# One level of Strassen's scheme in the down projection of a decoder layer, with the sums of operands made by accumulating DMAs

## The chip, the core and the metric

The kernel runs on one core of one Trainium2 chip. TensorE (PE in the rows, PEld for its weight loads) multiplies, VectorE (DVE), ScalarE (ACT) and GpSimd (POOL) do elementwise work, and 16 DMA engines move data for the queues of SyncE (SP), ACT and POOL. The metric is the device time of one execution in microseconds; lower is better. A measurement of this kernel tells two versions apart from about 0.5% on.

## The reference, cut to what matters

One layer: a mixer with three head groups, then a SwiGLU feed-forward network, then a final norm (its gain `norm_final`, one row per token). The change touches the feed-forward network's second product, with 512 tokens, width 1024 and `FFN_HIDDEN` 2816:

```
x = x + mix @ w_out
h = rmsnorm(x, norm_ffn)
gate, up = jnp.split(h @ w_gate_up, 2, axis=-1)
return x + (jax.nn.silu(gate) * up) @ w_down
```

Everything is float32.

## The kernel before

**Precision by splitting.** Each float32 operand of a large product is split into a high part `hi` (cast by ACT) and a rest `lo` (subtracted by DVE or POOL), and each product is three matmuls: hi·hi, hi·lo, lo·hi. Weights arrive as chunks of 256 rows by up to 512 columns (512 KB); `split` makes `hi` and `lo` of a chunk, from a ring of four buffers each, and `chunk()` keeps `LOOK` = 3 chunks split ahead of the one that TensorE uses.

**Stages.** The input projection and the mixer come first (to about 440 us), then the output projection (to about 480 us), then the gate and up projection (to 707.7 us), then the down projection with the final norm. The gate and up projection already runs as seven products of halves for each of six column blocks (five of 512 columns, one of 256). Its sums of weights are made partly by DVE, partly by DMAs that add what they bring to what stands in the destination (`add_chunk`, `accum_op=ALU.add`, issued on POOL's queue). When a buffer of the last block's weights comes free, `follow` brings a chunk of the down projection into it (`bring`, SP's queue): twelve buffers, `down_units`.

**Down projection before.** The activations, transposed by `turn` into 22 tiles `aT` of 128 rows by 512 tokens, are split by ACT and POOL (`split_t`). The loop runs over 11 chunk pairs in `DOWN_ORDER` and, inside, over four groups of 128 tokens; each step does twelve matmuls into two of eight PSUM banks (two column halves, two row tiles, three matmuls). The banks are first seeded with the residual `x2` by transposes. At the last chunk pair each token group is finished: square and sum on ACT, reciprocal root on POOL (`rsq`), scaling, and store. Four activation tiles are kept in DRAM (`ad`) for lack of room, and `x2` is brought back from DRAM (`x2d`) during the last gate and up block.

The order of instructions on each engine is settled by a scheduler at build time, not by the order of the code alone. Each engine, and each DMA queue's issuing engine, runs its own list in order: an instruction that waits holds up all that stand behind it on that engine.

Of the kernel before, what the change touches and what calls it, by code (L numbers as in the profile page):

```python
# [8 lines left out]
F32 = mybir.dt.float32  # L9
F32R = mybir.dt.float32r  # L10
# [6 lines left out]
P = 128  # L17
# [72 lines left out]
DOWN_ORDER = [2, 3, 4, 5, 6, 7, 8, 9, 10, 0, 1]  # L90
SPILL = 4
for _kc in DOWN_ORDER:
    for _g in range(2):
        CHUNKS.append(("down", 256 * _kc, np.arange(512 * _g, 512 * _g + 512)))
# [25 lines left out]
def trunk(tc, x, xt, wcat, vecs, rows, consts, posn, gfin, out):  # L120
# [6 lines left out]
    with contextlib.ExitStack() as es:  # L127
# [41 lines left out]
        for _, _, c in CHUNKS:  # L169
            offsets.append(o)  # L170
            o += P * 2 * len(c)
# [8 lines left out]

        def bring(i, t):

            w = len(CHUNKS[i][2])
            raw = t[:, 0:2 * w]
            sp.dma_start(
                out=raw,
                in_=wcat[offsets[i]:offsets[i] + P * 2 * w].rearrange("(p f) -> p f", p=P),
            )
            raws[i] = raw

        def add_chunk(i, t):

            w = len(CHUNKS[i][2])
            pool.dma_start(  # L194
                out=t[:, 0:2 * w],
                in_=wcat[offsets[i]:offsets[i] + P * 2 * w].rearrange("(p f) -> p f", p=P),
                accum_op=ALU.add,
            )
# [8 lines left out]
        def split(raw, eng, first=False):  # L207
# [5 lines left out]
            return v3(hi, 2), v3(lo, 2)  # L213
# [716 lines left out]

        def begin_ffn():
# [11 lines left out]
            def pair_jobs(p, U):  # L943
# [19 lines left out]
                def follow(unit, quarter=None):  # L963

                    if p + 1 < len(GU_W):
                        if quarter is not None:
                            gload(p + 1, quarter, unit)
                    else:
                        for t in unit:
                            down_units.append(t)  # L970
                            bring(DN0 + len(down_units) - 1, t)
# [40 lines left out]
            def down_job(j):  # L1012
                def run():
                    r_ = split(raws[DN0 + j], dve)
                    if DN0 + j + 12 < len(CHUNKS):
                        bring(DN0 + j + 12, down_units[j % 12])
                    return r_

                return run
# [5 lines left out]
            jobs.extend(down_job(j) for j in range(len(CHUNKS) - DN0))  # L1025
# [180 lines left out]
        aT = [None] * (2 * len(DOWN_ORDER))  # L1206
# [15 lines left out]
        def turn(p, f, a):  # L1222


            def go():
# [3 lines left out]
                kt = 4 * p + f  # L1229
                t = slot()  # L1230
                act.copy(out=t, in_=ps)
                if kt < SPILL:
                    sp.dma_start(out=ad[kt], in_=t)
                else:
                    aT[kt] = t
# [8 lines left out]
        for p, w in enumerate(GU_W):  # L1244
# [15 lines left out]
            if last:  # L1260
                for k in range(KD):
                    x2[k] = slot()
                    sp.dma_start(out=x2[k], in_=x2d[k])
# [12 lines left out]
            if last:  # L1276
                for hf in range(2):
                    gf[hf] = slot()
                    sp.dma_start(out=gf[hf], in_=gfin[512 * hf:512 * hf + 512].partition_broadcast(P))
# [19 lines left out]
        for k in range(SPILL):  # L1299
            aT[k] = slot()  # L1300
            sp.dma_start(out=aT[k], in_=ad[k])
        banks = [bank() for _ in range(4)]
        NK2 = len(DOWN_ORDER)
        asp = {}

        def split_t(n):
            if n < NK2:
                for kk in (2 * DOWN_ORDER[n], 2 * DOWN_ORDER[n] + 1):
                    hi, lo = slot(F32R), slot(F32R)
                    act.copy(out=hi, in_=aT[kk])  # L1310
                    pool.tensor_tensor(out=lo, in0=aT[kk], in1=hi.bitcast(F32), op=ALU.subtract)
                    asp[kk] = hi, lo

        split_t(0)
        split_t(1)


        order = [(n, c) for n in range(NK2) for c in range(NC)]
        order[3:5] = [(1, 0), (0, 3)]
        w2s = {}  # L1320
        for n, c in order:
            kc = DOWN_ORDER[n]
            if n not in w2s:
                w2s[n] = [chunk(), chunk()]
                split_t(n + 2)
            w2 = w2s[n]
            if n == 0 and c >= 2:
                banks += [mbank() for _ in range(2)]
            for hf in range(2):
                whi, wlo = w2[hf]  # L1330
                o_ = banks[2 * c + hf]
                if n == 0:
                    for k in range(4):
                        mm(o_[:, k * P:(k + 1) * P], lhsT=x2[4 * hf + k][:, c * P:(c + 1) * P], rhs=ident, start=k == 0, stop=False, is_transpose=True)
                for k in range(2):
                    ah, al = (t[:, c * P:(c + 1) * P] for t in asp[2 * kc + k])
                    mm(o_, lhsT=ah, rhs=whi[:, k, :], start=False, stop=False)  # L1337
                    mm(o_, lhsT=ah, rhs=wlo[:, k, :], start=False, stop=False)  # L1338
                    mm(o_, lhsT=al, rhs=whi[:, k, :], start=False, stop=n == NK2 - 1 and k == 1)  # L1339
            while (n, c) == (0, 2) and tail:  # L1340
                turn_one()
            if n == NK2 - 1:
                ss, rf = small(2, "ssf", bufs=4), small(1, "rf", bufs=4)
                t = [slot() for _ in range(2)]
                for hf in range(2):
                    o_ = banks[2 * c + hf]
                    act.activation(out=t[hf], in_=o_, func=AF.Square, accum_out=ss[:, hf:hf + 1])
                pool.tensor_scalar(out=ss[:, 0:1], in0=ss[:, 0:1], scalar1=1.0 / D, scalar2=EPS, op0=ALU.mult, op1=ALU.add)
                dve.scalar_tensor_tensor(out=rf, in0=ss[:, 1:2], scalar=1.0 / D, in1=ss[:, 0:1], op0=ALU.mult, op1=ALU.add)
                rsq(rf)  # L1350
                for hf in range(2):
                    y = slot()
                    dve.tensor_tensor(out=y, in0=banks[2 * c + hf], in1=gf[hf], op=ALU.mult)
                    if hf == 0:
                        act.activation(out=y, in_=y, func=AF.Copy, scale=rf)
                    else:
                        dve.tensor_scalar(out=y, in0=y, scalar1=rf, scalar2=None, op0=ALU.mult)
                    (act if hf else sp).dma_start(out=out[c, :, 512 * hf:512 * hf + 512], in_=y)
# [70 lines left out]
```

## Time and profile before

| | us |
|---|---|
| median of three runs (lowest to highest) | 840.64 (839.98 to 843.13) |
| the profiled execution | 839.7 |
| its span in the trace | 837.9 |
| TensorE busy | 825.2 |
| VectorE busy | 531.6 |
| ScalarE busy | 384.3 |
| GpSimd busy | 235.1 |

The span is the time from the first to the last instruction in the trace; the profiled execution's own time is 1.8 us longer than it. Matmuls overlap in their pipeline, so what one costs is the distance between the starts of two, not its recorded duration.

### The profile page before, as it was taken

Reading aid. Unit: us, or ns where it says so; the run is one execution under the profiler, and the core shown is the slowest. Engines: PE = TensorE matmul, PEld = TensorE weight load, DVE = VectorE, ACT = ScalarE, POOL = GpSimd, SP = SyncE. Lnnn points to the kernel's source line nnn. Section 1 sums busy time; section 2 is a strip of 40 time slices with the busy share of each in tenths; the row PEclk is TensorE's granted clock in tenths of the full one; section 3 lists DMA queues with packets and bytes.
Section 4 is the critical chain, followed back from the end, with each engine's and each line's share of the span. In section 5 each row is a group of like instructions: output and inputs, shape, how many; then the busy total and the mean of one; then the engine's idle time right before and its main releaser. Section 6 shows DMA issues by size and latency. Waiting matters only on the chain.

```text
span 837.9 us, 11283 instructions
## 1 busy us (share of the span) xinstructions
PE 825.2 (98%) x4238; PEld 711.0 (85%) x4238; DVE 531.6 (63%) x767; ACT 384.3 (46%) x659; POOL 235.1 (28%) x250
## 2 busy tenths in 40 slices
PE   9999999999999999999999999999999999999997
PEld 9989889898978788888888878888888889888885
DVE  6648757594839878556732797887878777422223
ACT  6344536463445454244422584646455557612223
POOL 3234524242012966531700221000010103850001
PEclk9999999999999999999999999999999999999999
DMA  7423242232313423213923579496665459330002
GB/s 256 158 60 125 83 141 87 95 113 65 125 63 91 147 77 126 76 59 116 328 76 106 158 228 262 132 270 176 185 188 143 99 151 388 114 118 0 1 1 100
DMA packets 38262, 110.72 MB, mean 132 GB/s; under 512 B 4392, under 2 KB 4776, under 8 KB 38208
## 3 DMA queue, kind: packets, MB, share of 16 engines
q1 hardware_dynamic: 33744, 96.93, 34.0%
q0 software_dynamic: 3456, 11.54, 7.7%
q10 hardware_dynamic: 1008, 1.54, 0.5%
q8 instruction: 33, 0.54, 0.3%
q14 instruction: 21, 0.17, 0.1%
HBM read 104.70 MB, written 5.29 MB: 131 GB/s over the span
## 4 chain that ended last, share of the span: by engine, by line
PE 62%; DVE 6%; POOL 1%; issue 1%; ACT 1%; DMA 0%; POOLq 0%; SPq 0%
PE b L1218 6%; PE b L1219 6%; PE b L1217 6%; PE b L428 4%; PE b L427 4%; PE b L429 4%; PE b L409 3%; PE b L411 3%; PE b L410 3%; PE b L1337 2%; PE b L1338 2%; PE b L1339 2%; PE m L1337 2%; PE m L1338 2%; PE m L1339 2%; PE m L1217 2%
## 5 line engine op out<-in xcount | busy, mean ns | idle before, releaser
L212 DVE TENSOR_TENSOR lo<-raw,hi 128x1024 fp32r<-128x1024 f32 (+3 forms) x97 | 117.2, 1212 | 116.5 <-ACT hi L211 116.0
L211 ACT CAST hi<-raw 128x1024 fp32r<-128x1024 f32 (+3 forms) x106 | 103.3, 977 | 155.1 <-PE b L428 75.8
L212 DVE TENSOR_TENSOR lo<-big,hi 128x1024 fp32r<-128x1024 f32 (+1 forms) x79 | 96.9, 1230 | 87.7 <-ACT hi L211 86.3
L211 ACT CAST hi<-big 128x1024 fp32r<-128x1024 f32 (+1 forms) x79 | 78.1, 991 | 112.8 <-PE m L1339 54.5
L427 PE MATMUL b<-s,hi 128*128 128x512 f32 x304 | 120.1, 396 | 0.8 <-ACT s L677 0.8
L428 PE MATMUL b<-s,hi 128*128 128x512 f32 x304 | 119.0, 392 | 0.0
L429 PE MATMUL b<-s,lo 128*128 128x512 f32 x304 | 118.5, 392 | 0.0
L410 PE MATMUL b<-lo,s 128*128 128x384 f32 (+2 forms) x320 | 115.3, 360 | 0.2 <-DVE lo L212 0.2
L409 PE MATMUL b<-hi,s 128*128 128x384 f32 (+2 forms) x320 | 114.1, 365 | 0.0
L411 PE MATMUL b<-hi,s 128*128 128x384 f32 (+2 forms) x320 | 113.6, 361 | 0.0
L1218 PE MATMUL b<-lo,s 128*128 128x512 f32 (+1 forms) x240 | 89.7, 374 | 1.2 <-DVE lo L212 1.2
L1219 PE MATMUL b<-hi,s 128*128 128x512 f32 (+1 forms) x240 | 89.3, 372 | 0.0
L1217 PE MATMUL b<-hi,s 128*128 128x512 f32 (+1 forms) x240 | 88.4, 378 | 0.0
L427 PEld LDWEIGHTS b<-s,hi 128*128 128x128 f32 x304 | 57.1, 188 | 12.1 <-ACT s L677 1.1
L429 PEld LDWEIGHTS b<-s,lo 128*128 128x128 f32 x304 | 57.1, 188 | 11.6
L428 PEld LDWEIGHTS b<-s,hi 128*128 128x128 f32 x304 | 57.2, 188 | 11.0
L410 PEld LDWEIGHTS b<-lo,s 128*128 128x128 f32 x320 | 60.2, 188 | 5.4 <-DVE lo L212 0.6
L409 PEld LDWEIGHTS b<-hi,s 128*128 128x128 f32 x320 | 60.1, 188 | 4.7 <-issue 0.2
L411 PEld LDWEIGHTS b<-hi,s 128*128 128x128 f32 x320 | 60.0, 188 | 4.9
L658 DVE SCALAR_TENSOR_TENSOR s<-s,vec,s 128x511 f32<-128x511 f32 (+2 forms) x66 | 58.5, 929 | 0.2 <-ACT s L655 0.2
L194 POOL DMA_DIRECT2D big<-in_wcat x19 | 16.8, 882 | 145.1 <-DMA big<-in_wcat 116.9
L1218 PEld LDWEIGHTS b<-lo,s 128*128 128x128 f32 x240 | 45.2, 189 | 9.4 <-DVE lo L212 1.6
(293 smaller groups left out, 1536.2 us busy)
## 6 DMA issues: line engine op xcount, KB each, us to landing
raw<-in_wcat SPq DMA_DIRECT2D x70, 512.0 KB, 3.4
big<-in_wcat SPq DMA_DIRECT2D x54, 512.0 KB, 4.4
big<-in_wcat POOLq DMA_DIRECT2D x17, 512.0 KB, 7.6
raw<-in_wcat SPq DMA_DIRECT2D x20, 384.0 KB, 3.1
s<-in_xt SPq DMA_DIRECT2D x16, 256.0 KB, 6.7
s<-mdr SPq DMA_DIRECT2D x12, 256.0 KB, 4.2
s<-adr SPq DMA_DIRECT2D x12, 256.0 KB, 5.0
x2d<-s SPq DMA_DIRECT2D x8, 256.0 KB, 3.2
```

The source lines that it names most:

```text
L211: pin(act.copy(out=hi, in_=raw), first)
L212: pin(eng.tensor_tensor(out=lo, in0=raw, in1=hi.bitcast(F32), op=ALU.subtract), first)
L409: mm(o_, lhsT=hh, rhs=whi[:, k, :], start=kk == 0, stop=False)
L410: mm(o_, lhsT=hh, rhs=wlo[:, k, :], start=False, stop=False)
L411: mm(o_, lhsT=hl, rhs=whi[:, k, :], start=False, stop=kk == KD - 1)
L427: mm(banks[t], lhsT=wh, rhs=rhs_hi[kk], start=a, stop=False)
L428: mm(banks[t], lhsT=wh, rhs=rhs_lo[kk], start=False, stop=False)
L429: mm(banks[t], lhsT=wl, rhs=rhs_hi[kk], start=False, stop=b)
L658: dve.scalar_tensor_tensor(out=a[:, sft:S], in0=u[:, 0:S - sft], scalar=w[3 - sft], in1=a[:, sft:S], op0=ALU.mult, op1=ALU.add)
L1217: mm(o_, lhsT=ah, rhs=whi[:, k, :], start=first and s_ == 0 and k == 0, stop=False, skip_group_check=not first)
L1218: mm(o_, lhsT=ah, rhs=wlo[:, k, :], start=False, stop=False, skip_group_check=not first)
L1219: mm(o_, lhsT=al, rhs=whi[:, k, :], start=False, stop=s_ == 1 and k == 1, skip_group_check=not first)
```

## The change

The down projection `a @ w_down` becomes seven products of halves. Tokens are halved (256 and 256), output columns are halved (512 and 512), and the 22 row tiles of the weights are halved by turns (even and odd tiles); `NJ` = 6 chunks cover one half of the rows, five of two tiles and one of one tile. Below, W11, W12, W21, W22 are the four quarters of the weights, by row half and column half (`down(0, 0, j)`, `down(0, 1, j)`, `down(1, 0, j)`, `down(1, 1, j)`); A11 and so on are the quarters of the activations, of which `turn` now writes `N11` (negative), `A21`, `A12` and `N22` (negative), each in six pieces.

- A product uses two token groups of 128, eleven row tiles and three matmuls for each: 66 matmuls. Seven products follow one another (`product7`), called products 1 to 7 here.
- Weights: W11 stands in units 0 to 5, W22 in units 6 to 11 of `down_units`. While product 1 runs, W12 is added by DMA onto units 6 to 11 (used by product 2) and onto units 0 to 5 (product 3); then W11 onto units 6 to 11 (product 4), W21 onto units 6 to 11 (product 7). W21 and W22 are brought into units 0 to 5 for products 5 and 6.
- Activations: `add_a21(j)` copies A21 to `SA` by a DMA of SP's queue and then adds N11 onto A21 by a DMA of POOL's queue; product 2 uses that sum. `add_s` adds N22, N11 and A12 onto `SA` by DMAs of POOL's queue, for products 3, 4 and 6. All these DMAs move from SBUF to SBUF, but four of the N22 pieces come from DRAM (`ad`).
- The rests `lo` of the activations are made by DVE, no longer by POOL. The results of products are combined by DVE. `x2` and the final gain are loaded after the first products instead of during the last gate and up block.
- The last product finishes its two token groups one after the other (`done`); the other two are finished beside it.

The diff, cut to its core:

```diff
-DOWN_ORDER = [2, 3, 4, 5, 6, 7, 8, 9, 10, 0, 1]
+NJ = 6
+for _h in range(2):
+    for _n in range(2):
+        for _j in range(NJ):
+            CHUNKS.append(("down", tuple(4 * _j + 2 * i + _h for i in range(2) if 4 * _j + 2 * i < FFN // P), np.arange(512 * _n, 512 * _n + 512)))
...
+        def add_a21(j):
+
+            SA[j] = slot(w=256 * nt(j))
+            sp.dma_start(out=SA[j], in_=A21[j])
+            pool.dma_start(out=A21[j], in_=N11[j], accum_op=ALU.add)
+
+        def add_s(j, n):
+
+            src = (N22[j] if j >= SPILL else ad[j], N11[j], A12[j])[n]
+            pool.dma_start(out=SA[j], in_=src, accum_op=ALU.add)
...
+                def after_11(j, t):
+                    add_chunk(down(0, 1, j), down_units[NJ + j])
+                    add_a21(j)
+                    add_chunk(down(0, 1, j), t)
+
+                for units, after in (
+                    (0, after_11),
+                    (NJ, lambda j, t: add_chunk(down(0, 0, j), t)),
+                    (0, lambda j, t: bring(down(1, 0, j), t)),
+                    (NJ, lambda j, t: add_chunk(down(1, 0, j), t)),
+                    (0, lambda j, t: bring(down(1, 1, j), t)),
+                    (0, None),
+                    (NJ, None),
+                ):
+                    for j in range(NJ):
+                        job(units, j, after)
...
-                t = slot()
-                act.copy(out=t, in_=ps)
...
+                two = ((N11, -1.0), (A21, 1.0)) if f % 2 == 0 else ((A12, 1.0), (N22, -1.0))
+                for hf, (q, sign) in enumerate(two):
+                    if f < 2:
+                        q[p] = slot(w=256 * nt(p))
+                    act.activation(out=q[p][:, 256 * (f // 2):256 * (f // 2) + 256], in_=ps[:, 256 * hf:256 * hf + 256], func=AF.Copy, scale=sign)
...
-        order = [(n, c) for n in range(NK2) for c in range(NC)]
...
+        seq7 = [(N11, -1.0), (A21, -1.0), (SA, 1.0), (SA, 1.0), (A12, 1.0), (SA, 1.0), (N22, -1.0)]
...
+                if 1 <= i // NJ <= 3:
+                    add_s(j, i // NJ - 1)
...
+        product7(0, b1, between=turn_last)
...
+        product7(1, b7)
+        w7 = pair_of(slot)
+        for c in range(2):
+            dve.tensor_tensor(out=w7[c], in0=b7[c], in1=s1[c], op=ALU.add)
...
+        product7(2, b5, src=[t[:, 256:512] for t in x2[4:8]])
+        b6 = pair_of(mbank)
+        product7(3, b6)
...
+        product7(4, b2, src=[t[:, 0:256] for t in x2[0:4]])
...
+        product7(5, b3, src=dx)
...
+        product7(6, b4, src=[t[:, 256:512] for t in x2[0:4]], done=last_quarter)
```

**POOL's queue.** Before, behind the last adding DMA of the gate and up projection (L194), POOL's list held the 22 subtractions that make the rests of the activations (L1311, split tiles `s`); the first five:

```order
L1311 TENSOR_TENSOR s_1184_6405<-s_982_5236,s_1183_6404 128x512
L1311 TENSOR_TENSOR s_1186_6409<-s_990_5279,s_1185_6408 128x512
L1311 TENSOR_TENSOR s_1188_6413<-s_998_5330,s_1187_6412 128x512
L1311 TENSOR_TENSOR s_1190_6417<-s_1006_5377,s_1189_6416 128x512
L1311 TENSOR_TENSOR s_1196_6431<-s_1032_5542,s_1195_6430 128x512
```

Now the same place holds adding DMAs: L203 is `add_chunk` (weights `in_wcat` onto a unit, `big` or `raw`), L951 the sum for A21, L956 a sum onto `SA`; 128x1024 is 512 KB, 128x512 is 256 KB, and x2 is two in a row.

```order
L203 DMA big_809_4295<-in_wcat 128x1024 x2
L203 DMA big_810_4296<-in_wcat 128x1024
L203 DMA raw_811_4297<-in_wcat 128x1024
L951 DMA s_933_4928<-s_932_4926 128x512
L956 DMA s_1161_6336<-ad_3885 128x512
L203 DMA big_808_4294<-in_wcat 128x1024 x2
L203 DMA big_809_4295<-in_wcat 128x1024
L951 DMA s_983_5239<-s_982_5237 128x512
L956 DMA s_1164_6361<-ad_3885 128x512
L203 DMA raw_812_4298<-in_wcat 128x1024
L951 DMA s_1033_5550<-s_1032_5548 128x512
L956 DMA s_1167_6382<-ad_3885 128x512
```

The list goes on without a gap:

```order
L203 DMA big_808_4294<-in_wcat 128x512
L203 DMA raw_813_4299<-in_wcat 128x1024
L951 DMA s_1083_5861<-s_1082_5859 128x512
L956 DMA s_1178_6423<-ad_3885 128x512
L203 DMA big_810_4296<-in_wcat 128x1024
L203 DMA big_810_4296<-in_wcat 128x512
L951 DMA s_1133_6172<-s_1132_6170 128x512
L956 DMA s_1183_6448<-s_1142_6215 128x512
L203 DMA big_809_4295<-in_wcat 128x1024 x2
L203 DMA big_810_4296<-in_wcat 128x1024
L203 DMA raw_811_4297<-in_wcat 128x1024
L951 DMA s_1186_6471<-s_1185_6469 128x256
```

The six L951 rows are the sums for the six pieces of A21. The last of them (`s_1186`) has moved behind the first four adds of W11 onto units 6 to 9, which belong to product 4.

**ACT, in product 2.** Before, ACT's list at this point of the down projection held only casts of weights (L211), two for each of the eleven steps:

```order
L211 CAST hi_1239_6797<-big_809_4295 128x1024
L211 CAST hi_1241_6801<-raw_812_4298 128x1024
L211 CAST hi_1247_6861<-raw_813_4299 128x1024
L211 CAST hi_1249_6865<-big_810_4296 128x1024
L211 CAST hi_1255_6925<-big_810_4296 128x1024
```

Now casts of weights (L216) alternate with the high parts of the activations of product 2 (L1356) and product 3 (L1353):

```order
L216 CAST hi_1225_6615<-big_808_4294 128x1024
L1356 ACTIVATE s_1219_6588<-s_1033_5550 128x512
L1356 ACTIVATE s_1223_6610<-s_1083_5861 128x512
L216 CAST hi_1229_6637<-big_808_4294 128x512
L216 CAST hi_1233_6659<-big_808_4294 128x1024
L1356 ACTIVATE s_1227_6632<-s_1133_6172 128x512
L216 CAST hi_1237_6681<-big_809_4295 128x1024
L216 CAST hi_1241_6703<-raw_812_4298 128x1024
L1356 ACTIVATE s_1231_6654<-s_1186_6471 128x256
L1353 CAST s_1235_6676<-s_1161_6336 128x512
L1353 CAST s_1239_6698<-s_1164_6361 128x512
```

The cast for the last piece of product 2 reads `s_1186`, the sum that stands last in the fence above, and all casts of product 3's activations stand behind it.

**DVE, at the end.** Before, the last token group's `rf` (L1349) stood ahead of the product with the gain (L1353) on the same engine:

```order
L1353 TENSOR_TENSOR s_1295_7213<-m_1213_6544,s_1157_6264 128x512
L1349 SCALAR_TENSOR_TENSOR rf_1292_7205<-ssf_1291_7204 128x1
L1353 TENSOR_TENSOR s_1296_7217<-m_1214_6545,s_1158_6266 128x512
L1357 TENSOR_SCALAR s_1296_7217<-s_1296_7217,rf_1292_7205 128x512
L1425 UNCONDITIONAL_BRANCH
```

Now the sum of the last bank (L1465) comes first, and both products with the gain (L1397) stand ahead of `rf` (L1401):

```order
L1465 TENSOR_TENSOR s_1244_6715<-m_1370_7296,s_1244_6715 128x512
L1397 TENSOR_TENSOR s_1388_7397<-s_1243_6714,s_1245_6718 128x512
L1401 SCALAR_TENSOR_TENSOR rf_1386_7392<-ssf_1385_7391 128x1
L1397 TENSOR_TENSOR s_1391_7418<-s_1302_6987,s_1246_6720 128x512
L1397 TENSOR_TENSOR s_1392_7422<-s_1244_6715,s_1245_6718 128x512
L1401 SCALAR_TENSOR_TENSOR rf_1390_7417<-ssf_1389_7416 128x1
```

One sum and one product with the gain have moved between the last matmul and the last `rf`.

## Rows read from the trace of the kernel before

**Rows 1.** The page: busy times; granted clock, DMA share in 40 slices.

```profile
PE 825.2 (98%) x4238; PEld 711.0 (85%) x4238; DVE 531.6 (63%) x767; ACT 384.3 (46%) x659; POOL 235.1 (28%) x250
PEclk9999999999999999999999999999999999999999
DMA  7423242232313423213923579496665459330002
```

**Rows 2.** Waits of PE: engine, line, waited for, us in total, times, longest.

```profile
PE m L868 <- DVE s L823: 1.3, 1, 1.3
```

**Rows 3.** Groups of PE, 708 to 832 us, first of six alike.

```profile
L1337 PE MATMUL b<-hi,s 128*128 128x512 f32 x88 | 34.7, 394 | 0.0
```

**Rows 4.** PE in order of time, down projection: start, duration; first and last.

```profile
707.75 0.60 PE L1334 MATMUL b<-kst,s 128*128 128x128 f32 x4
...
825.70 0.39 PE L1338 MATMUL b<-lo,s 128*128 128x512 f32 x1
...
831.37 0.39 PE L1339 MATMUL m<-hi,s 128*128 128x512 f32 x1
```

**Rows 5.** Groups of ACT (708 to 832) and DVE (600 to 832).

```profile
L211 ACT CAST hi<-big 128x1024 fp32r<-128x1024 f32 x14 | 14.7, 1052 | 54.5 <-PE m L1339 54.5
L1310 ACT CAST s<-s 128x512 fp32r<-128x512 f32 x20 | 11.0, 620 | 0.0
...
L212 DVE TENSOR_TENSOR lo<-big,hi 128x1024 fp32r<-128x1024 f32 x37 | 49.6, 1341 | 72.3 <-ACT hi L211 71.6
L212 DVE TENSOR_TENSOR lo<-big,hi 128x512 fp32r<-128x512 f32 x11 | 7.6, 688 | 4.0 <-ACT hi L211 4.0
```

**Rows 6.** The end in order of time, ACT, DVE, POOL, last token group.

```profile
831.16 0.69 DVE L1353 TENSOR_TENSOR s<-m,s 128x512 f32<-128x512 f32 x1
...
833.40 0.72 ACT L1355 ACTIVATE s<-s,rf 128x512 f32<-128x512 f32 x1 [0.93 <-POOL rf L286]
```

**Rows 7.** Stretches: us, busy by engine, granted clock, DMA share, GB/s.

```profile
544.00:546.00 2.00, 2.00 (x11) 1.63 (x10) 1.97 (x2) 0.64 (x2) 0.00 (x0) 1.00 1.04 203
550.00:552.00 2.00, 2.00 (x10) 1.65 (x9) 2.00 (x4) 0.58 (x1) 0.86 (x1) 1.00 1.05 420
553.00:563.00 10.00, 10.00 (x48) 8.29 (x47) 6.32 (x8) 4.92 (x7) 0.86 (x1) 1.00 1.04 270
```

**Rows 8.** DMA issues in order of time around 544, POOL's, then SP's.

```profile
540.57 0.93 POOL L194 DMA_DIRECT2D big<-in_wcat  x1 [21.10 <-DMA big<-in_wcat]
541.79 0.86 POOL L194 DMA_DIRECT2D big<-in_wcat  x1 [0.29 <-issue]
...
539.45 0.33 SPq L1233 DMA_DIRECT2D ad<-s  x1
543.42 0.33 SPq L185 DMA_DIRECT2D big<-in_wcat  x1
```

**Rows 9.** DMA queues of the whole span: packets, MB, share of 16 engines.

```profile
q1 hardware_dynamic: 33744, 96.93, 34.0%
q0 software_dynamic: 3456, 11.54, 7.7%
```

**Rows 10.** DMA issues of the page: count, KB, median us to landing.

```profile
big<-in_wcat SPq DMA_DIRECT2D x54, 512.0 KB, 4.4
big<-in_wcat POOLq DMA_DIRECT2D x17, 512.0 KB, 7.6
```

**Rows 11.** SP's issues in order of time, end of the gate and up projection.

```profile
695.41 1.77 SPq L185 DMA_DIRECT2D big<-in_wcat  x2
...
698.35 0.33 SPq L185 DMA_DIRECT2D big<-in_wcat  x1
```

**Rows 12.** Stretches, instructions of L300 alone, then stretches at the end.

```profile
3.00:5.00 2.00, 2.00 (x12) 2.00 (x11) 1.00 0.96 322
6.50:7.50 1.00, 1.00 (x11) 1.00 (x11) 1.00 1.04 361
...
836.00:838.00 2.00, 0.00 (x0) 0.00 (x0) 0.00 (x0) 0.00 (x0) 0.00 (x0) 0.50 0.10 38
```

More of the change, by code (lines that the diff above doesn't have):

```diff
@@ L929, in trunk, with down, nt @@
         down_units = []
+        def down(h, n, j):
+            return DN0 + (2 * h + n) * NJ + j
+        def nt(j):
+            return len(tiles_of(CHUNKS[down(0, 0, j)]))
+        N11, A21, A12, N22, SA = ([None] * NJ for _ in range(5))
+        def add_a21(j):
[5 more added lines that the diff above has]
+            pool.dma_start(out=SA[j], in_=src, accum_op=ALU.add)
         def begin_ffn():
@@ L1024, in begin_ffn @@
                 jobs.extend(order)
-            jobs.extend(down_job(j) for j in range(len(CHUNKS) - DN0))
+            down_jobs()
             gload(0, R11, roles["r11"])
@@ L1296, in trunk @@
             tail.extend(turn(p, f, e + u) for f in range(w // P))
[L1299 to L1312, printed above, removed]
@@ L1314, in trunk @@
-        split_t(0)
-        split_t(1)
-        order = [(n, c) for n in range(NK2) for c in range(NC)]
[L1319 to L1358, printed above, removed]
@@ new lines, in seed, with product7 @@
+        def seed(o_, src, c):
+            for k in range(4):
+                mm(o_[:, k * P:(k + 1) * P], lhsT=src[k][:, c * P:(c + 1) * P], rhs=ident, start=k == 0, stop=False, is_transpose=True)
+        def product7(m, banks, src=None, between=None, done=None):
+            wts = []
+            for j in range(NJ):
+                split_next()
+                wts.append(chunk())
+                if done and j == NJ - 2:
+                    continue
+                for c in range(2):
+                    o_ = banks[c]
+                    if src and j == 0:
+                        seed(o_, src, c)
+                    for jj in ((j - 1, j) if done and j == NJ - 1 else (j,)):
+                        (whi, wlo), (ahi_, alo_) = wts[jj], asp[m * NJ + jj]
+                        for k in range(nt(jj)):
+                            ah, al = (t[:, k, c * P:(c + 1) * P] for t in (ahi_, alo_))
+                            a, b = not src and jj == 0 and k == 0, jj == NJ - 1
+                            mm(o_, lhsT=ah, rhs=whi[:, k, :], start=a, stop=False)
+                            mm(o_, lhsT=ah, rhs=wlo[:, k, :], start=False, stop=False)
+                            mm(o_, lhsT=al, rhs=whi[:, k, :], start=False, stop=b)
+                    if done and j == NJ - 1:
+                        done(c)
+                tick()
+                if between:
+                    between(j)
@@ new lines, in pair_of, with turn_last @@
+        def pair_of(make):
+            return [make() for _ in range(2)]
+        split_next()
+        split_next()
+        b1 = pair_of(bank)
+        def turn_last(j):
+            if j == 1:
+                while tail:
+                    turn_one()
+        product7(0, b1, between=turn_last)
+        s1 = pair_of(slot)
+        for c in range(2):
+            act.copy(out=s1[c], in_=b1[c])
+        for k in range(KD):
+            x2[k] = slot()
+            sp.dma_start(out=x2[k], in_=x2d[k])
@@ new lines, in trunk @@
+        b7 = pair_of(bank)
+        product7(1, b7)
+        w7 = pair_of(slot)
+        for c in range(2):
+            dve.tensor_tensor(out=w7[c], in0=b7[c], in1=s1[c], op=ALU.add)
+        for hf in range(2):
+            gf[hf] = slot()
+            sp.dma_start(out=gf[hf], in_=gfin[512 * hf:512 * hf + 512].partition_broadcast(P))
+        b5 = pair_of(mbank)
+        product7(2, b5, src=[t[:, 256:512] for t in x2[4:8]])
+        b6 = pair_of(mbank)
+        product7(3, b6)
+        e, c22 = pair_of(slot), pair_of(slot)
@@ new lines, in trunk @@
+        for j in range(SPILL):
+            N22[j] = slot()
+            sp.dma_start(out=N22[j], in_=ad[j])
+        b2 = pair_of(bank)
+        product7(4, b2, src=[t[:, 0:256] for t in x2[0:4]])
+        for c in range(2):
+            dve.tensor_tensor(out=s1[c], in0=b2[c], in1=s1[c], op=ALU.add)
+        b3 = pair_of(bank)
+        product7(5, b3, src=dx)
+        for c in range(2):
+            dve.tensor_tensor(out=e[c], in0=b3[c], in1=e[c], op=ALU.add)
+            finish_half(c, s1[c], e[c])
```

121 lines of the change are left out of this document (74 added, 47 removed).

## Prediction

> **What bounds the kernel now.** I read the page first: TensorE is busy for 98% of the span and its granted clock is at the upper of its two levels, 2.4 GHz, in all 40 slices, while the DMA engines are nearly idle in the last eight of them [rows 1]. Then the waits: the longest that TensorE has anywhere is 1.3 us [rows 2]. So a stretch ends when its matmuls end, and nothing but matmuls is worth saving as long as operands come in time. Then the down projection itself. It is six groups of 88 matmuls of 512 columns, 528 in all [rows 3], from the seeds at 707.75 to the last start at 831.37 us; from 825.70 to 831.37 the starts of 25 matmuls in a row lie 5.67 us apart, 0.2267 us each [rows 4]. 528 of these make 119.7 us, and with 40 transposes (32 seeds and 8 of `turn`, four in about 0.35 us by the distance of their starts) 123 of the 124 us are accounted for. The span ends 6.5 us after the last start, 6.15 us after that matmul's end.
>
> **What is saved.** Seven products of 66 matmuls are 462; 66 fewer, at 0.2267 us, save 15.0 us. The seeds stay 32.
>
> **What lies beside.** A product takes 66 x 0.2267 = 15.0 us of TensorE. Its splits take 5.5 x 1.05 + 5.5 x 0.62 = 9.2 us of ACT and, with 1.34 and 0.69, 11.2 us of DVE [rows 5]. Both fit under the product, and the weights run three chunks ahead. DVE's combinations add at most eight pieces of 0.69 us in one product, 16.7 us against 15.0 once, which that lead takes up. If the cover went, each product would cost the difference, so I book nothing. The second copy in `turn` falls on ACT, busy for 46% of the span [rows 1]. GpSimd loses 22 subtractions and gains DMA issues of 0.86 us [rows 8]; the 27 that count below take 23 us, less than their data.
>
> **What an adding DMA costs.** Between 544 and 546 us two adding DMAs of 512 KB, issued at 540.57 and 541.79, run almost alone: the engines are full (share 1.04) and move 203 GB/s. Between 550 and 552 plain loads fill them as well (1.05) and move 420 GB/s [rows 7, 8]. So 512 KB (0.524 MB) cost all 16 engines 2.6 us when they are added and 1.25 us when they are loaded. When both kinds are queued they share the same engines: from 553 to 563 the share is 1.04 and the rate 270 GB/s, between the two [rows 7]. The averages over the whole span are higher: 11.54 MB in 7.7% of 837.9 us is 2.93 us for 512 KB added, 96.93 MB in 34.0% is 1.54 us for 512 KB loaded [rows 9]. I use these as the two ends of the price.
>
> The Trainium skill ("DMA: Bandwidth & Descriptors", section "Anatomy of one DMA — SWDGE (gpsimd) path") gives a DMA on this path about 2.0 us plus its bytes at 436 GB/s, so 1.2 us of moving for 512 KB, with no surcharge for adding. The trace does not agree, at 2.6 us; by the page the sums would come about as early as in the first rival.
>
> **What waits for them.** Product 2 needs, for each of its six chunks, a unit with W12 added and a piece of A21 with N11 added. The last piece of A21 is the last row of the POOL queue that the section on the change prints. The queue runs in order, so ahead of it and with it move, counted in those rows: adds of weights, 14 of 512 KB and 2 of 256 KB, that is 15 of 512 KB; sums of activations, 10 of 256 KB and one of 128 KB, that is 10.5. By bytes that is 15 x 2.6 + 10.5 x 1.3 = 52.7 us of full engines, or 15 x 2.93 + 10.5 x 1.47 = 59.4 at the higher price. SP's plain transfers share the engines meanwhile: 3.5 loads of W22 still to come, 5.5 copies to `SA` and eight loads of `x2` (256 KB each), and about two loads of W21: (3.5 + 2) x 1.25 + 13.5 x 0.63 = 15.4 us, or 18.9 at the higher price. The sum is 68 to 78 us. Saturated engines should run near the lower end, but the stretch from 553 to 563 moved two adds and some 1.65 MB of loads, which the low price makes 9.1 us, in 10 us. I take 72.
>
> The queue cannot begin before the first W22 unit has been loaded. Its buffer comes free at 695.4, where the load of the seventh down chunk is issued now [rows 11]; it lands 4.4 us later [rows 10], and with the issue of 0.86 us the first add moves at about 701. So the last piece of A21 lands at 701 + 72 = 773 us.
>
> **When TensorE wants it.** Product 1 starts at 707.75 and takes 15.0 us and 0.7 of `turn`, so product 2 could end at 738.5. It has one chunk left when the piece lands: split by ACT and DVE (about 1.1 us at half width, with hand-overs), then six matmuls, 1.4 us. It ends at 775.5, 37 us late. ACT's list holds all of product 3's activations behind that split, so nothing overtakes.
>
> **After that.** Products 3 to 7 take 330 x 0.2267 = 74.8 us, and 16 of the 32 seed transposes still lie in them (1.4 us; the others stand inside product 2's wait). The next sums follow in the queue: half a sum, 1.5 adds of weights, 5.5 sums and some 4.5 loads of W21, 17 to 20 us, so the last lands at about 793. Product 4 starts at about 793 and needs that one 12 us later. That cover holds with 10 us to spare. The clock: 12 matmuls of L300 fit into the two us from 3 to 5, and 11 into the one from 6.5, so at first they cost about twice as much; at the end the granted clock is at 0.50, the 1.2 GHz level, from 836 on, after the last matmul at 831.4 [rows 12, 4]. Ahead of product 2's last chunk stand four adds and one and a half sums, 12.4 us, so TensorE idles some 9 us there, longer than it does before the clock is seen low at the end. I take it that it comes back slow as at the start, where it was slow from 1 to about 6 us, and book half of that, 2.5 us, once.
>
> The Trainium skill ("TensorE: Matmul & The Clock Gate", section "HAM oscillation — how this bites in real kernels") describes bursts of matmuls between waits for DMA that each start at the slow clock. Here that would also touch the earlier chunks of product 2, but those are waited for anyway; no row of this trace shows a fall inside the kernel.
>
> **The end.** Behind the last matmul DVE now first adds the bank (0.69 us), and one product with the gain (0.69 us) stands ahead of `rf` [rows 6]: 6.15 + 1.4 = 7.55 us.
>
> **The sum.** 775.5 + 2.5 + 74.8 + 1.4 + 7.55 = 861.8 us of span, against 837.9. The profiled execution is 1.8 us above its span and the median 0.9 above that: 864 us.
>
> **Rivals.**
> - *The sums come almost in time* (faster). If adding DMAs moved as fast as loads, the queue would take 15 x 1.25 + 10.5 x 0.63 + 15.4 = 40.8 us, the piece would land at 742, and product 2 would end at 744.3, 6 us late: 837.9 - 15.0 + 6 + 1.4 = 830.3, 833 us as a median. It decides at the point where the delay eats the 13.6 us that are left: a queue of 48 us instead of 72. For it speaks that the engines are idle otherwise [rows 1]; against it 203 GB/s at full engines [rows 7], and 7.6 us to landing against 4.4 [rows 10]. Chance 5%.
> - *The later sums are late too.* If POOL, held up by one of its waits, issues product 4's sums 18 us later than I reckon, the 10 us of cover are gone and 8 us are added: 872 us. Chance 12%.
> - *Sums inside SBUF are cheap.* No row shows an add whose source is SBUF. If it costs what a copy costs, 0.63 us, the queue is 7 us shorter: 857; with the low price for all else 4 more, 853. Nothing speaks for less. Chance 18%.
>
> **How the numbers follow.** The forecast has 62%, its own range 858 to 870 (queue of 68 to 78 us). The range of 851 to 874 takes in the cheap and the late case and leaves out the first rival and the worst of the late ones. Half a per cent, 4.2 us, is about what a measurement of this kernel can tell from no change. Faster is the first rival, 5%; 3% lie within half a per cent, where the adds would cost about 1.6 us for 512 KB; slower 92%.
>
> **What would show it.** After the change TensorE should wait in product 2 for splits that wait for DMAs onto `s`, some 35 us in all, the last time for over 8 us; the DMA share should stand near full from 701 to 790 at about 250 GB/s; product 2 should end at 773 to 783 and the last five products run without a wait, 15 us each; the granted clock should fall once. A wait for DMA in products 3 to 7, or a DMA rate above 300 GB/s while sums are queued, would prove a step wrong; product 2 ending before 750 would prove the whole wrong.

## The result, and the profile after

The kernel after takes 869.23 us (median of four runs, 866.69 to 870.47) against 840.31 us before (838.77 to 843.13): a ratio of 1.0336, 95% interval 1.03 to 1.0373. It is slower by 29 us; the forecast was 864, range 851 to 874. The profiled execution took 866.69 us, its span is 864.8 us.

From the page of the kernel after: the granted clock and the busy share of the DMA engines, in tenths, in 40 slices of 21.6 us, and one row of the table of queues (packets, MB, share of 16 engines over the span).

```profile
PEclk9999999999999999999999999999999998769998
DMA  6523232422234242128425695967755589999902
q0 software_dynamic: 10368, 28.84, 18.4%
```

Against [rows 1], the last eight slices have turned round: the DMA engines, nearly idle there before, are full from about 700 to 820 us, and TensorE's clock dips. GpSimd's queue q0 moves 28.84 MB where [rows 9] had 11.54; the 17.30 MB more are the new sums.

The waits of the stretch from 700 to 866 (us in total, times, longest us), and from the timeline every matmul that waited over 0.5 us behind 705 (start, duration; in brackets the idle time ahead of it and what ended it):

```profile
ACT s L1356 <- DMA s<-s: 39.5, 5, 12.6
PE b L1382 <- ACT s L1356: 29.4, 6, 12.1
POOL s L956 <- DVE s L1354: 18.6, 2, 15.6
```

```profile
719.11 0.50 PE L1382 MATMUL b<-hi,s 128*128 128x512 f32 x1 [0.77 <-ACT s L1356]
734.08 0.80 PE L1382 MATMUL b<-hi,s 128*128 128x512 f32 x1 [7.88 <-ACT s L1356]
741.32 0.50 PE L1382 MATMUL b<-hi,s 128*128 128x512 f32 x1 [1.75 <-ACT s L1356]
749.83 0.79 PE L1382 MATMUL b<-hi,s 128*128 128x512 f32 x1 [5.50 <-ACT s L1356]
756.32 0.50 PE L1382 MATMUL b<-hi,s 128*128 128x512 f32 x1 [1.38 <-ACT s L1356]
772.97 0.79 PE L1382 MATMUL b<-hi,s 128*128 128x512 f32 x1 [12.07 <-ACT s L1356]
...
816.43 0.50 PE L1384 MATMUL b<-hi,s 128*128 128x512 f32 x1 [1.52 <-DVE s L1354]
```

The first row is the fifth chunk of product 1, whose split waits for no DMA. The next five are the chunks 2 to 6 of product 2, 28.6 us in all. Each waits for ACT's split of a piece of A21 (L1356, the line of the splits of products 1, 2 and 7), and ACT waits for the DMA onto that piece (`s<-s`, five times). Before, the longest wait was 1.3 us [rows 2]. The last row is in product 5, after 28 of its 66 matmuls; the timeline of PE and DVE around it:

```profile
812.08 1.04 PE L1364 MATMUL m<-kst,s 128*128 128x128 f32 x8
812.61 1.42 DVE L1449 TENSOR_TENSOR s<-s 128x256 f32<-128x256 f32 x4
812.87 0.47 PE L1382 MATMUL b<-hi,s 128*128 128x512 f32 x1
...
813.88 1.03 PE L1364 MATMUL b<-kst,s 128*128 128x128 f32 x8
...
815.68 1.29 DVE L1354 TENSOR_TENSOR s<-s,s 128x512 fp32r<-128x512 f32 x2
```

L1364 are the seeds of products 7 and 6, which the scheduler has put here; L1354 makes the rests of the activations, and L1449 makes the four pieces of `dx`, the difference of `x2` that seeds product 6.

The chain of waits says how the DMAs of product 2 follow one another (start, duration, what):

```profile
700.79 14.64 DMA s<-s
...
716.51 18.89 DMA s<-ad
...
735.94 15.86 DMA big<-in_wcat
...
753.48 19.00 DMA s<-s
```

From 701 to 772.5 the end of the kernel hangs on transfers, one behind the other, each 15 to 19 us from issue to landing. The first is a copy of A21 to `SA` in SP's queue, for which the sum onto that piece has to wait; the other three stand in GpSimd's queue, and the last of them is the last sum of A21. Stretches (length, busy us and count of PE, PEld, DVE, ACT, POOL, then granted clock, DMA share, GB/s):

```profile
701.00:772.50 71.50, 42.61 (x196) 34.06 (x195) 27.20 (x35) 23.76 (x37) 25.01 (x29) 0.82 1.07 249
710.00:720.00 10.00, 9.23 (x44) 7.32 (x43) 5.95 (x8) 4.91 (x10) 6.05 (x8) 1.00 1.08 253
730.00:740.00 10.00, 5.49 (x12) 3.85 (x12) 4.28 (x4) 4.42 (x6) 3.43 (x4) 0.50 1.09 256
747.00:753.50 6.50, 3.67 (x9) 2.90 (x10) 2.52 (x3) 2.08 (x3) 2.59 (x4) 0.50 1.10 207
760.00:770.00 10.00, 0.90 (x9) 0.67 (x7) 1.23 (x1) 0.68 (x1) 0.00 (x0) 0.70 1.05 261
772.90:777.80 4.90, 4.83 (x12) 3.80 (x12) 3.79 (x6) 2.91 (x6) 1.74 (x2) 0.51 1.03 190
800.00:820.00 20.00, 18.48 (x90) 15.25 (x90) 16.30 (x25) 12.77 (x19) 0.00 (x0) 1.00 1.05 297
820.00:840.00 20.00, 20.00 (x90) 16.58 (x89) 13.50 (x17) 7.96 (x8) 0.00 (x0) 1.00 0.01 3
```

Up to 772.5 the engines are full at 249 GB/s on the average, near the 270 of the mixed stretch in [rows 7]; they are done only at 820. The end, from the timeline (to be read beside [rows 6]):

```profile
854.72 0.61 PE L1384 MATMUL m<-hi,s 128*128 128x512 f32 x2
855.15 1.29 DVE L1465 TENSOR_TENSOR s<-m,s 128x512 f32<-128x512 f32 x2 [4.10 <-PE m L1384]
855.87 0.63 ACT L1396 ACTIVATE s<-s 128x512 f32<-128x512 f32 x1 [6.83 <-DVE s L1465]
...
857.11 0.61 ACT L1396 ACTIVATE s<-s 128x512 f32<-128x512 f32 x1
...
859.03 0.72 ACT L1403 ACTIVATE s<-s,rf 128x512 f32<-128x512 f32 x1 [1.21 <-POOL rf L291]
...
859.93 0.72 ACT L1403 ACTIVATE s<-s,rf 128x512 f32<-128x512 f32 x1 [0.18 <-issue]
```

The last two matmuls belong to two banks, so both banks are complete only there, the two L1465 additions follow one another, and two finishes of a row block stand one behind the other: 9.5 us from the end of the last matmul (855.33) to the end of the span.

### The profile page after: what moved, and what is told of

Read it like the earlier page. It is cut to its first block, busy times and chain, and to the rows that moved or that the text cites. A ratio compares the mean times of both kernels' runs of the same rounds, so it can differ in the third digit from the quotient of the medians.

```text
span 864.8 us, 11426 instructions
## 1 busy us (share of the span) xinstructions
PE 818.3 (95%) x4172; PEld 703.4 (81%) x4172; DVE 576.7 (67%) x849; ACT 412.9 (48%) x723; POOL 245.2 (28%) x276
## 3 DMA queue, kind: packets, MB, share of 16 engines
q0 software_dynamic: 10368, 28.84, 18.4%
## 4 chain that ended last, share of the span: by engine, by line
PE 53%; DMA 8%; DVE 7%; issue 2%; POOL 1%; ACT 1%; SPq 0%; ACTq 0%; POOLq 0%; DVEq 0%
PE b L1267 5%; PE b L1268 5%; PE b L1266 5%; DMA s<-s 4%; PE b L433 4%; PE b L432 4%; PE b L434 4%; PE b L414 3%; PE b L416 3%; PE b L415 3%; DMA s<-ad 2%; DVE lo L217 2%; PE m L1266 2%; PE m L1267 2%; PE m L1268 2%
## 5 line engine op out<-in xcount | busy, mean ns | idle before, releaser
L217 DVE TENSOR_TENSOR lo<-raw,hi 128x1024 fp32r<-128x1024 f32 (+3 forms) x102 | 120.8, 1188 | 109.9 <-ACT hi L216 109.9
L216 ACT CAST hi<-raw 128x1024 fp32r<-128x1024 f32 (+3 forms) x111 | 108.5, 980 | 153.0 <-PE b L433 79.3
L217 DVE TENSOR_TENSOR lo<-big,hi 128x1024 fp32r<-128x1024 f32 (+1 forms) x94 | 107.1, 1144 | 44.7 <-ACT hi L216 44.6
L216 ACT CAST hi<-big 128x1024 fp32r<-128x1024 f32 (+1 forms) x94 | 90.6, 967 | 86.2 <-PE b L1268 30.2
L203 POOL DMA_DIRECT2D big<-in_wcat x38 | 33.7, 895 | 192.2 <-DMA big<-in_wcat 112.1
L415 PEld LDWEIGHTS b<-lo,s 128*128 128x128 f32 x320 | 60.2, 188 | 4.8
L1382 PE MATMUL b<-hi,s 128*128 128x512 f32 x88 | 36.2, 426 | 29.4 <-ACT s L1356 29.4
```

What stands on the lines that cost most here:

```text
L415: mm(o_, lhsT=hh, rhs=wlo[:, k, :], start=False, stop=False)
```

## The experiments

The theory: adding DMAs cost the engines twice a load's time, and all that stands in the queue ahead of the last sum of A21 delays product 2 by its bytes times that price. The rivals: it is latency and order on GpSimd's queue, not the price; sums inside SBUF are cheap; order alone is to blame. Ratios are to the kernel before.

**Three kernels that take the adding away.** In the first every adding DMA of the down stage becomes plain, in the second only those of the weights, in the third only those of the activations (the sums concerned are left out). The first line of this diff is changed in the first and the second, the other two in the first and the third:

```
-            pool.dma_start(out=t[:, 0:WIDTH[i]], in_=chunk_of(i), accum_op=ALU.add)
+            more = {} if i >= DN0 else dict(accum_op=ALU.add)
+            pool.dma_start(out=t[:, 0:WIDTH[i]], in_=chunk_of(i), **more)
-            pool.dma_start(out=A21[j], in_=N11[j], accum_op=ALU.add)
+            pool.dma_start(out=A21[j], in_=N11[j])
-            pool.dma_start(out=SA[j], in_=src, accum_op=ALU.add)
+            pool.dma_start(out=SA[j], in_=src)
```

> Every adding DMA of the down stage is a plain DMA of the same bytes on the same queue in the same order (so the sums of weights and activations are left out, nothing else). Capacity theory (512 KB added cost the engines 2.6 us and loaded 1.25): the queue up to the last sum of A21 shrinks from 70.5 us to about 41, that piece lands at about 742 instead of 772, product 2 ends at about 744 and the span is 864.8 - 30 = about 835 (time about 837). Latency theory (it is the queue's order, issue and landing times, not the bytes' price, that make the piece late): the piece lands within some 8 us of 772 and the span stays above 855.

> Only the weights' adding DMAs of the down stage become plain loads (those sums are left out); the sums of activations stay. Capacity theory: 15 x (2.6 - 1.25) = 20 us less queue ahead of the last sum of A21, which lands at about 752; span about 845. If sums inside SBUF cost only what a copy costs: 8 us better still for both this and the kernel after, so the difference stays 20. If it is the sums of activations that make it late: span above 858.

> Only the sums of activations become plain copies (those sums are left out); the weights' adding DMAs stay. Capacity theory with equal prices for equal bytes: 10.5 x (1.3 - 0.63) = 7 us less queue, the last A21 piece lands at about 765, span about 858. If a sum whose source is SBUF already costs only what a copy costs, the span stays at 863 to 866; if it costs more than one from DRAM, the span is below 854.

Measured: 843.08 us (ratio 1.0031, 1.0011 to 1.005), 846.72 (1.0082, 1.0052 to 1.0112) and 861.57 (1.0259, 1.0229 to 1.0289); spans 842.2, 846.0 and 859.3. In the chains of waits of the three, the transfer that brings the last piece of A21:

```profile
736.38 11.37 DMA s<-s
```

```profile
743.43 10.79 DMA s<-s
```

```profile
750.40 17.16 DMA s<-s
```

It lands at 747.8, 754.2 and 767.6, where 742, 752 and 765 were expected, against 772.5 with all sums. The latency theory falls: the same DMAs in the same order, without the adding, bring it 25 us earlier. In the second and the third kernel it lands 2 to 3 us behind what was expected, in the first 6: there too the engines are full (share 1.02 to 1.04, 393 to 400 GB/s from 710 to 750), so this change would have waited for its transfers even at a load's price. The rows of q0 in the three tables of queues give the price itself:

```profile
q0 software_dynamic: 8448, 28.84, 13.4%
```

```profile
q0 software_dynamic: 10112, 28.84, 15.1%
```

```profile
q0 software_dynamic: 8704, 28.84, 16.4%
```

The bytes are the same, the shares of the spans are 112.9, 127.7 and 140.9 us of full engines, and 159.1 in the kernel after. Adding the 22 x 512 KB of weights thus costs 159.1 - 127.7 = 31.4 us more than loading them, or 140.9 - 112.9 = 28.0 us where the activations are plain too: 1.27 to 1.43 us for 512 KB (the prediction had 2.6 - 1.25 = 1.35). Adding the 22 x 256 KB of activations costs 18.2 us more than copying them, or 14.8 where the weights are plain too: 0.67 to 0.83 us for 256 KB (it had 0.67). All but four of these sums have their source in SBUF, and they are not cheap: byte for byte they cost about as much extra as the weights'.

**Another order on the queue.** The same DMAs; W12 onto the W11 units moves into product 2's jobs, W11 onto the W22 units into product 3's, and `pin` holds the order (in the sums of activations too).

```
-            pool.dma_start(out=t[:, 0:WIDTH[i]], in_=chunk_of(i), accum_op=ALU.add)
+            d = pool.dma_start(out=t[:, 0:WIDTH[i]], in_=chunk_of(i), accum_op=ALU.add)
+            pin(d, i >= DN0)
...
                 def after_11(j, t):
                     add_chunk(down(0, 1, j), down_units[NJ + j])
                     add_a21(j)
-                    add_chunk(down(0, 1, j), t)
+                def after_22(j, t):
+                    add_chunk(down(0, 1, j), down_units[j])
+                def after_s(j, t):
+                    add_chunk(down(0, 0, j), down_units[NJ + j])
+                    bring(down(1, 0, j), t)
...
-                    (NJ, lambda j, t: add_chunk(down(0, 0, j), t)),
-                    (0, lambda j, t: bring(down(1, 0, j), t)),
+                    (NJ, after_22),
+                    (0, after_s),
```

> The same DMAs with the same bytes in another order on POOL's queue: for each product only the sums that it needs, in the order of need (W12 onto the W22 units and A21 first, W12 onto the W11 units in product 2, W11 onto the W22 units in product 3). Capacity theory: 5.5 x 2.6 + 5.5 x 1.3 + about 8 us of plain transfers stand ahead of the last A21 piece, which lands at about 731 to 735, before product 2 wants it; the rest is late later by about 10 us for product 3 and some 12 for product 4 together, and the span is about 843 to 847. If only the total of bytes matters (the last of them lands at about 798 to 812 whatever the order, and the products wait for it), the span stays above 858. If order is all and the price nothing: about 833.

Measured: 866.45 us (1.0317, 1.0287 to 1.0347), span 864.9. A miss, by 18 us: no faster than the kernel after, and where the theory that only the total matters had put it (above 858). From its timelines of PE and ACT, then from its waits of PE:

```profile
822.42 1.22 PE L1389 MATMUL b<-hi,s 128*128 128x512 f32 x2 [8.03 <-ACT hi L217]
...
819.97 0.40 ACT L1360 CAST s<-s 128x256 fp32r<-128x256 f32 x1 [4.02 <-DMA s<-s]
```

```profile
PE b L1389 <- ACT hi L217: 8.0, 1, 8.0
PE m L1389 <- ACT hi L217: 6.6, 3, 4.8
PE m L1371 <- DMA s<-x2d: 2.9, 2, 1.5
PE b L1371 <- DMA s<-x2d: 1.9, 2, 1.4
```

Product 2's wait is gone (its chunks wait under 1 us), but product 6 cannot start before 822: ACT waits until 820 for the last sum of activations, which now stands behind sums of W21 that only product 7 wants, and product 6's first cast of weights (L217) stands behind that on ACT. Products 3 and 4 wait 6.6 us for casts of weights, and seeds wait 4.8 us for `x2`. Product 6's wait was a flaw of the experiment's order, and it made the next one: those sums of W21 go last.

```
+                def after_12(j, t):
+                    add_chunk(down(1, 0, j), down_units[NJ + j])
+                    bring(down(1, 1, j), t)
...
-                    (NJ, lambda j, t: add_chunk(down(1, 0, j), t)),
-                    (0, lambda j, t: bring(down(1, 1, j), t)),
+                    (NJ, None),
+                    (0, after_12),
```

> The first kernel with another order held product 6 until 820 us, since its last activation sum stood behind the six sums of W21 that only product 7 wants. Here these six go to the end of the queue; all else is as there. Capacity theory: 5.5 x 2.6 = 14.3 us of weights' sums now stand behind that last activation sum instead of ahead of it, so it lands at about 806 instead of 820, product 6 starts 14 us earlier, the six weights' sums still land by about 820, before product 7 wants them, and the span is 848 to 853. If the order on the queue has nothing to do with it and only the total of bytes counts, the span stays at 862 to 866.

Measured: 854.62 us (1.0175, 1.0153 to 1.0196), span 852.5, inside the range of the capacity theory. So order on the queue is worth about 12 us of span: product 6 no longer waits for a sum. What this order does not remove is the total: the engines are still full up to 820, and TensorE still waits 5.9 us for casts of weights and 5.5 us for `x2`.

```profile
800.00:820.00 20.00, 17.94 (x83) 14.37 (x82) 16.27 (x27) 9.11 (x15) 0.00 (x0) 1.00 1.02 265
```

**The activations' sums on an engine.** VectorE adds them (all is computed); D = A21 + N11 goes to a new buffer and the other sums run on in A21's own, which does without the six copies.

```
             SA[j] = slot(w=256 * nt(j))
-            sp.dma_start(out=SA[j], in_=A21[j])
-            pool.dma_start(out=A21[j], in_=N11[j], accum_op=ALU.add)
+            dve.tensor_tensor(out=SA[j], in0=A21[j], in1=N11[j], op=ALU.add)
...
-            pool.dma_start(out=SA[j], in_=src, accum_op=ALU.add)
+            if n == 0 and j < SPILL:
+                pool.dma_start(out=A21[j], in_=src, accum_op=ALU.add)
+            else:
+                dve.tensor_tensor(out=A21[j], in0=A21[j], in1=src, op=ALU.add)
...
-        seq7 = [(N11, -1.0), (A21, -1.0), (SA, 1.0), (SA, 1.0), (A12, 1.0), (SA, 1.0), (N22, -1.0)]
+        seq7 = [(N11, -1.0), (SA, -1.0), (A21, 1.0), (A21, 1.0), (A12, 1.0), (A21, 1.0), (N22, -1.0)]
```

> The sums of activations on VectorE (0.69 us each for 512 columns) instead of by adding DMAs: the sum of A21 and N11 goes to a new buffer and the other sums run on in A21's own, so the six copies fall away too; four sums, those with the spilled N22 from DRAM, stay adding DMAs. All is computed. Capacity theory: 18 x 1.3 us of adding and 3.5 us of copies leave the engines, some 27 of 110 us, and the last sum of A21 no longer stands behind weights in a queue: product 2 starts without a wait of over 4 us, the DMA share falls from full at about 785 to 795 instead of 820, and the span is 826 to 836 with VectorE's 18 x 0.69 us as the new cost. If the weights' sums alone saturate the engines up to the last products, the span stays above 845.

Measured: 833.42 us (0.9923, 0.9909 to 0.9938), span 832.5: 0.8% faster than the kernel before, and inside the range. The same sums on GpSimd (`pool.` for `dve.` in the two sums):

> As the kernel with the sums on VectorE, but on GpSimd, which is otherwise idle here. Capacity theory: the same 27 us leave the DMA engines; GpSimd needs 1.1 to 2 us for each sum in the queue that also issues the weights' adding DMAs, so some of these go out later; span 826 to 840. If VectorE is the bound of the other version, this one is faster by 2 us or more; if issue order on GpSimd is, it is slower.

Measured: 846.87 us (1.01, 1.0071 to 1.013), span 842.9: outside the range. From the groups of DVE between 700 and 770 (busy us, mean ns), first with the sums on VectorE, then on GpSimd, there with one row of DVE's timeline (start, duration):

```profile
L1356 DVE TENSOR_TENSOR s<-s,s 128x512 fp32r<-128x512 f32 x12 | 7.8, 682 | 0.0
L217 DVE TENSOR_TENSOR lo<-big,hi 128x512 fp32r<-128x512 f32 x6 | 4.1, 686 | 3.0 <-ACT hi L216 3.0
```

```profile
L1356 DVE TENSOR_TENSOR s<-s,s 128x512 fp32r<-128x512 f32 x11 | 13.7, 1279 | 0.0
L217 DVE TENSOR_TENSOR lo<-big,hi 128x512 fp32r<-128x512 f32 x5 | 12.1, 2410 | 1.2 <-ACT hi L216 1.2
...
701.60 7.43 DVE L217 TENSOR_TENSOR lo<-big,hi 128x512 fp32r<-128x512 f32 x1 [1.02 <-ACT hi L216]
```

VectorE's own instructions took 1.3 us instead of 0.68, and 2.4 instead of 0.69 (mean of five, one of them 7.43), while GpSimd was adding; TensorE waited 9.0 us for such splits (L217) and 2.8 us for another instruction of VectorE. It waited for no DMA, so the other explanation in the text above, that issue order on GpSimd is the bound, does not show in its waits. The Trainium skill ("SBUF — State Buffer", section "Who interferes with whom") says that a VectorE instruction with two inputs in SBUF contends with a GpSimd instruction that reads SBUF. The trace agrees: L1356 and L217 have two such inputs.

**Both together, and the ceiling.** First the activations' sums on VectorE with the weights' sums in the first of the two orders above; then a kernel without any sum or copy for one in the down stage (all are left out):

> Sums of activations on VectorE and the weights' adding DMAs in the order of need, held in that order. Capacity theory: with some 89 us of transfers from 701 on, the last sum that product 3 wants lands at about 745 and product 4's at about 766, so the waits are under 4 us together: span 826 to 832. If order matters nothing even now, it equals the version with the sums on VectorE alone within 2 us.

> No sums at all in the down stage, neither of weights nor of activations, and no copies for them (all of these are left out); everything else as in the kernel after. This is what seven products cost when their operands are simply there: 837.9 - 15.0 for the 66 matmuls, + 1.4 to 3.3 at the end, and at most 3 us of hold in product 6: span 824 to 830. If it is 835 or more, the change has a cost beside the sums that I have not named.

Measured: 832.69 us (0.9918, 0.9903 to 0.9933), span 831.1, and 831.4 us (0.9902, 0.9887 to 0.9917), span 829.8. With the activations off the queue the order matters no more than 1.4 us of span, and 1.3 us are left between this kernel and one with no sums at all; both lie inside their ranges. In the first of the two the engines are full until 790 and then done, while TensorE waits 3.9 us in all:

```profile
740.00:780.00 40.00, 39.32 (x181) 31.89 (x180) 33.91 (x48) 22.40 (x32) 6.89 (x8) 1.00 1.06 258
780.00:790.00 10.00, 8.50 (x41) 6.88 (x41) 10.00 (x18) 6.16 (x11) 0.00 (x0) 1.00 1.03 352
790.00:810.00 20.00, 20.00 (x90) 16.56 (x89) 13.52 (x15) 10.24 (x16) 1.40 (x2) 1.00 0.03 10
```

**The end and VectorE's queue.** The kernel after with the last 18 matmuls held in written order (the three `mm` of a tile alike), and then the version with VectorE's sums and the order of need, with that and with `dx` on GpSimd:

```
-                            mm(o_, lhsT=ah, rhs=whi[:, k, :], start=a, stop=False)
+                            pin(mm(o_, lhsT=ah, rhs=whi[:, k, :], start=a, stop=False), done and j == NJ - 1)
...
-            dve.tensor_tensor(out=dx[k], in0=x2[4 + k][:, 0:256], in1=x2[4 + k][:, 256:512], op=ALU.subtract)
+            pool.tensor_tensor(out=dx[k], in0=x2[4 + k][:, 0:256], in1=x2[4 + k][:, 256:512], op=ALU.subtract)
```

> The kernel after, with the last 18 matmuls held in the order in which they are written: the nine of the third row block's bank, then the nine of the fourth's. (In the kernel after they are interleaved, both banks are complete only with the last two matmuls, and the two finishes stand one behind the other.) If that is why the end measures 9.45 us behind the last matmul instead of 7.55, the end shrinks to 7.2 to 7.8 us and the span by about 2 us, to some 863. If the finish itself is longer than I reckoned, the end stays above 9 us.

> The version with the activations' sums on VectorE and the weights' sums in the order of need, with two things more: the last 18 matmuls held in written order, and the four subtractions of x2 (dx) on GpSimd instead of VectorE. If the end behind the last matmul and VectorE's queue ahead of product 6 are what remains (9.3 us and a hold of some 2 us), the span falls from 831.1 by 2 to 4 us, to 827 to 829, below the kernel with no sums at all; if VectorE is the bound throughout, only the end shrinks.

Measured: 866.5 us (1.0315, 1.03 to 1.033), span 864.0, and 832.57 us (0.9913, 0.9898 to 0.9928), span 830.1. The first moved its end to 8.4 us behind the last matmul (855.64), a little over half of the way, and not to 7.2 to 7.8. From its timeline, why no more:

```profile
855.80 0.68 DVE L1465 TENSOR_TENSOR s<-m,s 128x512 f32<-128x512 f32 x1
...
856.63 0.72 ACT L1403 ACTIVATE s<-s,rf 128x512 f32<-128x512 f32 x1 [0.92 <-POOL rf L291]
...
857.26 0.61 ACT L1396 ACTIVATE s<-s 128x512 f32<-128x512 f32 x1
```

The fourth row block's sum is there at 856.48, but ACT first scales the third's output, and squares at 857.26: 0.8 us, the rest of the difference. The second kernel gained 1.0 us of span, not 2 to 4, and its median shows no difference to the version without it. The hold by VectorE that the texts above place in or ahead of product 6 is in product 5 (see the row at 816.43 above); without `dx` on VectorE it is 0.9 us instead of 1.5, so `dx` was a part of it.

## Why the prediction was right

The change does what the forecast said, for the reason it gave.

- *66 matmuls fewer, 15.0 us.* Right. With no sums to wait for, the span falls by 8.1 us (837.9 to 829.8); of the other 6.9, 3.6 are the longer end (9.8 against 6.15), 1.5 the hold in product 5, which that kernel shows too, and the rest stays open.
- *The price of adding.* Right in kind and in size, by the three plain versions: 1.27 to 1.43 us extra for 512 KB of weights against 1.35. The first rival falls with them, and more than was said: it put the time at 833 us, but even at a load's price the kernel takes 843. Its plain transfers fill the engines until 750, so that the last piece lands at 747.8 instead of 742, and the hold and the longer end, told below, come on top.
- *Sums inside SBUF are cheap.* Refuted (0.67 to 0.83 us extra for 256 KB).
- *The queue up to the last A21 piece, 72 us from 701, landing at 773.* It landed at about 772.5, with its wait the last and longest, 12.07 us where 9 were expected; product 2 ended at 775.7, as forecast to 0.2 us. So close a fit is in part luck: 72 was taken between 68 and 78, the engines moved 17.8 MB (71.5 us at 249 GB/s) where the count gives 17.0, and a third load of W21 and two of the final gain were issued in that time, which the count leaves out. The five waits of product 2 come to 28.6 us, not 35; matmuls at the lower clock between them fill most of the rest. The last split took 0.5 us, not 1.1.
- *Later sums have cover.* Right: products 3 to 7 wait for no DMA. GpSimd was held up 15.6 us ahead of product 4's sums, which is the late case's mechanism, but the cover was enough. The engines stayed full until 820, not 790.
- *The clock falls once, 2.5 us.* It fell three times in product 2; [rows 12] had shown only start and end. I take it that only the last fall cost anything, since behind the slow matmuls of the other two TensorE waited for a DMA again (1.75 and 1.38 us): in the 4.9 us from 772.9 (granted clock 0.51) eleven matmuls started at about 0.44 us each instead of 0.2267, 2.3 us. The Trainium skill ("TensorE: Matmul & The Clock Gate", section "HAM oscillation — how this bites in real kernels") describes this pattern, bursts between DMA waits that start slow; here the trace agrees with it for three of the five bursts behind DMA waits, while two start at the upper level.
- *VectorE's combinations, booked at nothing.* Here a term was missing: the lead of three chunks did not take them up, and product 5 waited 1.52 us for L1354. Besides the eight combinations that the forecast counts, VectorE had the four subtractions of `dx` (L1449, 1.42 us) ahead of that split, which it leaves out.
- *The seeds.* By the starts in the rows above, one group of eight takes 0.8 us (812.08 to 812.87), the other, with the hold behind it, 2.55 us (813.88 to 816.43): 3.3 us together instead of 1.4.
- *The end, 7.55 us.* Mis-sized: 9.5, as two finishes ran together. Holding the matmuls' order won 1.1 us of it.

The terms add up: 861.8 - 0.5 (landing) - 0.6 (last split) - 0.2 (clock) + 0.5 (the 336 matmuls from there on, 76.7 us instead of 76.2) + 1.9 (seeds and hold) + 1.9 (end) = 864.8 us, the span. The median lies 2.5 us above the profiled execution, where the forecast took 0.9.

## What to carry to other kernels

A stretch with idle DMA engines is no free adder: price an adding DMA from a row where such DMAs run alone at full engines, add up all that stands ahead of the one that is waited for, then ask separately whether the total ends before the last consumer. Sums whose operands lie in SBUF belong on an engine that has room: moving 20 activation sums (0.68 us for 512 columns) to VectorE turned a change that costs 29 us into one that wins about 6. Before two engines share such work, look at whether one slows the other.

## What was not expected

- An adding DMA from SBUF to SBUF costs the engines no less than one from DRAM: 0.67 to 0.83 us extra for 256 KB against 1.27 to 1.43 for 512 KB.
- VectorE's 512-column subtraction L217, 0.69 us by itself, took 2.4 us on average (one of five 7.4) with GpSimd's additions beside it, and these took 1.7 to 2.2 us themselves.
- With the total of transfers unchanged, an order that freed product 2 of its wait gave all of it back in later waits, the longest of them 8.0 us ahead of product 6 (span 864.9), and moving six sums to the end gained 12 us.
